# Longer pacing in the side work of a decoder layer, low parts on another engine, attention in rounds of two key blocks

## The chip, the core and the metric

The kernel runs on one core of a Trainium2 chip. Its engines work at the same time, each through its own list of instructions in order: TensorE (PE: matrix products, and transposes as products with an identity), VectorE (DVE), ScalarE (ACT), GpSimd (POOL) and SyncE (SP, which issues the transfers, DMAs). An instruction waits until what it reads is written and the buffer that it writes is free, and everything behind it in its engine's list waits too. The metric is the time of one execution in microseconds (us), as the median of several runs.

## What is computed

One layer of a hybrid decoder, 1024 tokens of width 1024 in f32:

```python
u = rmsnorm(h, norm_mix)
(... q, k, v, gates of three branches ..., mg) = split_cols(u @ w_in, IN_SIZES)
y_a = gated_deltanet(...)          # 4 heads, chunks of 64, a triangular solve per chunk
y_b = mlstm(...)                   # 4 heads, chunks of 64
y_c = nsa(...)                     # 8 heads: compressed, selected and window attention
br = einsum('bsnc,ncd->bsnd', stack([y_a, y_b, y_c]), w_branch)
merged = sum(sigmoid(mg) * br)
h = h + merged @ w_out
gt, up = split(rmsnorm(h, norm_ffn) @ w_ffn_in, 2)
h = h + (silu(gt) * up) @ w_ffn_out
h = h + sigmoid(rmsnorm(h, norm_ple) @ w_ple_gate) * (p @ w_ple_proj)
```

The window branch sees the last 512 tokens, the selected branch up to four key blocks of 64 per query; three sigmoid gates per head weigh the three outputs. The delta rule needs the inverse of a unit lower triangular 64x64 matrix for each head and chunk.

## The kernel before

**Products.** Every large product is made of three in a rounded format. Each factor is split into a high part (ScalarE copies it into the rounded type) and a low part (the difference), and hi x hi + hi x lo + lo x hi is accumulated in PSUM. So `mm<-u,whi` and `mm<-u,wlo` in the profile are products of the activations with the high and the low part of a weight tile. Weights come by DMA in tiles of 128x512 (`wraw`, four buffers); `halve` in `run_blocks` makes `whi` on ScalarE (L429) and `wlo` on GpSimd (L431), into five buffers each. In the last phase every second `wlo` is made on VectorE.

**Three phases.** (1) The input projection, block by block, with the side work of the branches woven in: the delta rule's solve (`gdn_solve`) and scan, the mLSTM, the preparation of the attention. (2) The attention (`nsa_attend`), woven into ten blocks of the merge gates (`mg_block`). (3) The remaining merge gates, the branch projections, the output projection, the feed-forward network (FFN) and the gated embedding (PLE), without side work. The FFN multiplies blocks with seven products in place of eight: the function around L1755 (called the combine here) first forms sums of activation blocks (`uw`), and `part` makes high and low parts of them (`utT1h`, `utT1l` and so on, L1763 and L1764).

**The order.** Side work is written as generators. After each step of a block `advance` adds 1.4 us to a counter, `woven`, and lets the generators issue a few pieces. `yield from self.pause(us)` makes a generator sit still until `woven` has grown by that much. So a pause puts more of the blocks' products between one piece and the next in the engines' lists; it is no wait on the chip. A scheduler then fixes the order of each engine's list before the program runs. In phase 3, `self.later(lag, fn)` holds back the issue of some work until so many us of products have been issued.

**The solve.** For each head, `gdn_solve` transposes keys and queries (`ktr`, after `g_junk`, L838), forms `gram`, inverts the 16x16 diagonal blocks on VectorE by substitution (`zb`, `xb`, L893 and L894), which takes two trips through DRAM (`zds`, `xds`) and ends in `gV` on GpSimd and `gW` on VectorE (both L908). After `pause(14.0)` the doubling follows: levels of 64x64 products, `levq`, `levv` and `levw`, which put the inverse together from the blocks. In the preparation of the attention `khtr` transposes keys (`nsa_keys`, L1261).

**The attention.** For each block of 128 queries there are four tasks: the window and the selected branch, each in two halves of the heads (`hp`). `att_query` normalises and splits the queries (`qstk`, L1387 and L1388) and transposes them (`qtr`). `att_scores` forms scores `S` and exponentials `P` with their sums `n_sum`, and scales P by gate / sum (L1476 and L1478). `att_values` works on the task before: for each key block it transposes four P tiles into one PSUM bank (`ptr`, tag "pt", two banks), copies the bank to `PT` (ScalarE and VectorE in turn, from a pool of ten buffers), and one key block later adds the products with the values to `nso`, two products of 64 columns' width. At the end the compressed branch adds `nso<-PT,cv`, two products of 64x64. `nsa_attend` interleaves the pieces of scores and values.

**FFN and PLE.** `put` makes high and low parts, `ahi` (ScalarE, L1795) and `alo` (GpSimd, L1796), of the activations for the down product. In the PLE, `evac` multiplies (VectorE, L1965), adds the residual on GpSimd (L1967) and stores. `load_y` loads a branch's output and splits it into `yhi` and `ylo` on ScalarE and VectorE at once.

## Time and profile before

| | us |
|---|---|
| median of three runs (2393.13 to 2399.14) | 2394.88 |
| the execution whose profile is shown | 2392.93 |
| its span, first to last instruction | 2391.1 |

The mean granted TensorE clock over the span is 0.987 of full speed. The stages, from the windows of the trace (busy us of each engine):

| stage | from, to (us) | PE | DVE | ACT | POOL | clock |
|---|---|---|---|---|---|---|
| input projection with side work | 0 to 880 | 826.87 | 411.25 | 298.22 | 255.32 | 0.97 |
| attention with merge gates | 880 to 1311 | 410.35 | 321.94 | 212.41 | 107.22 | 1.00 |
| merge gates, branch projections | 1311 to 1480 | 164.84 | 86.78 | 46.92 | 43.67 | 1.00 |
| output projection, norm | 1480 to 1580 | 96.06 | 59.77 | 43.20 | 22.27 | 0.99 |
| combine and FFN | 1580 to 2298 | 703.20 | 414.00 | 220.37 | 309.53 | 0.99 |
| PLE | 2298 to 2391.1 | 84.90 | 44.49 | 35.13 | 44.88 | 0.99 |

How to read the lines below: a line names the line of the kernel, the engine, the operation, out<-in, the shape and the count ("x4"). In a group the busy time, the mean ns of one, and the idle time before it with its releaser follow. In a timeline the start and the duration stand ahead, in us. In a window the length stands first, then busy us and instructions of PE, its weight loads (PEld), DVE, ACT and POOL, then the granted clock, the DMA share and GB/s. A product of f32 operands, such as `nso`, stands in the trace as two passes for each product of the instruction list.

### The profile page before, as it was taken

Reading aid. Unit: us, or ns where it says so; the run is one execution under the profiler, and the core shown is the slowest. Engines: PE = TensorE matmul, PEld = TensorE weight load, DVE = VectorE, ACT = ScalarE, POOL = GpSimd, SP = SyncE. Lnnn points to the kernel's source line nnn. Section 1 sums busy time; section 2 is a strip of 40 time slices with the busy share of each in tenths; the row PEclk is TensorE's granted clock in tenths of the full one; section 3 lists DMA queues with packets and bytes.
Section 4 is the critical chain, followed back from the end, with each engine's and each line's share of the span. In section 5 each row is a group of like instructions: output and inputs, shape, how many; then the busy total and the mean of one; then the engine's idle time right before and its main releaser. Section 6 shows DMA issues by size and latency. Waiting matters only on the chain.

```text
span 2391.1 us, 34586 instructions
## 1 busy us (share of the span) xinstructions
PE 2286.2 (96%) x12840; PEld 1829.4 (77%) x12840; DVE 1338.2 (56%) x3088; ACT 856.3 (36%) x1832; POOL 782.9 (33%) x662
## 2 busy tenths in 40 slices
PE   8989898989999998999999999998999999999999
PEld 6777677878778996666665778986777777777789
DVE  5455555643223436888775446677555555555583
ACT  6424242423222334545454322452222222222362
POOL 2342424322122123322121151235444444444434
PEclk9999999999999999999999999999999999999999
DMA  6131212121122123111111643311111111111143
GB/s 230 50 96 40 92 40 65 59 64 45 63 77 80 45 93 107 58 54 45 50 45 50 228 164 129 128 57 36 53 49 54 49 49 51 51 53 53 53 133 128
DMA packets 121887, 183.05 MB, mean 77 GB/s; under 512 B 25275, under 2 KB 47204, under 8 KB 121720
## 3 DMA queue, kind: packets, MB, share of 16 engines
q1 hardware_dynamic: 121432, 180.72, 22.5%
q8 instruction: 101, 1.65, 0.3%
q14 instruction: 66, 0.54, 0.1%
q10 hardware_dynamic: 288, 0.14, 0.0%
HBM read 149.04 MB, written 31.76 MB: 76 GB/s over the span
## 4 chain that ended last, share of the span: by engine, by line
PE 77%; DVE 12%; issue 4%; POOL 3%; DMA 3%; ACT 2%; SPq 0%; POOLq 0%; ACTq 0%; DVEq 0%
PE mm L242 60%; PE nso L242 3%; PE ptr L250 2%; PE S L242 2%; POOL wlo L431 2%; DVE P L1478 1%; DVE zb L893 1%; DVE xb L894 1%; PE mops L242 1%; PE gks L242 1%; PE gpu L242 1%; ACT g_junk L838 1%; POOL alo L1796 1%; ACT whi L429 1%; PE levq L242 1%
## 5 line engine op out<-in xcount | busy, mean ns | idle before, releaser
L431 POOL TENSOR_TENSOR wlo<-wraw,whi 128x512 fp32r<-128x512 f32 x334 | 449.7, 1351 | 1063.9 <-ACT whi L429 818.9
L242 PE MATMUL mm<-u,whi 128*128 128x512 f32 x1888 | 632.7, 410 | 2.0 <-ACT mg L1606 2.0
L429 ACT ACTIVATE whi<-wraw 128x512 fp32r<-128x512 f32 x408 | 255.7, 630 | 470.2 <-PE mm L242 384.0
L242 PEld LDWEIGHTS mm<-u,whi 128*128 128x128 f32 x1888 | 341.4, 190 | 76.0 <-issue 11.5
L242 PE MATMUL mm<-u,wlo 128*128 128x512 f32 x944 | 379.2, 402 | 0.0
L242 PEld LDWEIGHTS mm<-u,wlo 128*128 128x128 f32 x944 | 178.3, 189 | 39.4 <-issue 1.2
L1839 DVE TENSOR_TENSOR fc<-fc,mm 128x512 f32<-128x512 f32 x140 | 95.3, 686 | 159.0 <-PE mm L242 158.9
L1880 DVE TENSOR_TENSOR h<-h,mm 128x512 f32<-128x512 f32 x176 | 118.6, 684 | 74.6 <-PE mm L242 72.1
L242 PE MATMUL mm<-whi,alo 128*128 128x512 f32 x352 | 141.6, 402 | 6.8 <-POOL alo L1796 6.8
L242 PE MATMUL mm<-whi,ahi 128*128 128x512 f32 x352 | 140.7, 400 | 5.5 <-ACT whi L429 5.5
L242 PE MATMUL mm<-wlo,ahi 128*128 128x512 f32 x352 | 140.6, 399 | 2.5 <-POOL wlo L431 2.5
L431 POOL TENSOR_TENSOR wlo<-ws,whi 128x512 fp32r<-128x512 f32 x60 | 84.3, 1405 | 148.7 <-ACT whi L429 148.7
L242 PE MATMUL mm<-u2hi,whi 128*128 128x512 f32 x304 | 121.1, 398 | 0.0
L242 PE MATMUL mm<-u2lo,whi 128*128 128x512 f32 x304 | 121.1, 398 | 0.0
L242 PE MATMUL mm<-u2hi,wlo 128*128 128x512 f32 x304 | 120.3, 396 | 0.0
L1472 ACT ACTIVATE P<-P,n_ng 128x640 f32<-128x640 f32 (+7 forms) x128 | 93.0, 728 | 64.1 <-DVE n_ng L1470 61.1
L429 ACT ACTIVATE whi<-ws 128x512 fp32r<-128x512 f32 x60 | 37.8, 630 | 174.9 <-DVE h L1880 130.4
L250 PE MATMUL ptr<-ident,P 128*128 128x128 f32 x528 | 89.8, 282 | 7.3 <-DVE P L1478 5.5
L250 PEld LDWEIGHTS ptr<-ident,P 128*128 128x128 f32 x528 | 59.6, 140 | 47.2 <-issue 28.3
L242 PE MATMUL mm<-whi,u 128*128 128x256 f32 x512 | 94.1, 283 | 0.1
L431 DVE TENSOR_TENSOR wlo<-wraw,whi 128x512 fp32r<-128x512 f32 x74 | 69.5, 939 | 35.5 <-ACT whi L429 35.4
L242 PEld LDWEIGHTS mm<-whi,alo 128*128 128x128 f32 x352 | 66.8, 190 | 27.2 <-POOL alo L1796 11.6
(497 smaller groups left out, 5048.9 us busy)
## 6 DMA issues: line engine op xcount, KB each, us to landing
wraw<-in_w_dram SPq DMA_DIRECT2D x408, 256.0 KB, 2.7
mgs<-mg SPq DMA_DIRECT2D x48, 256.0 KB, 2.3
mgld<-mgs SPq DMA_DIRECT2D x48, 256.0 KB, 5.6
xt<-in_x_dram SPq DMA_DIRECT2D x8, 512.0 KB, 4.8
xt<-in_x_dram SPq DMA_DIRECT2D x32, 128.0 KB, 3.7
sg<-pps SPq DMA_DIRECT2D x32, 128.0 KB, 3.5
out_dram<-sg SPq DMA_DIRECT2D x32, 128.0 KB, 2.8
pps<-ppst SPq DMA_DIRECT2D x8, 256.0 KB, 2.0
```

What stands on the lines that cost most here:

```text
L242: return self.nc.tensor.matmul(out, lhsT, rhs, start=start, stop=stop).ins
L250: self.nc.tensor.transpose(out, in_, self.ident[:n, :n])
L429: nc.scalar.activation(hi, t, AF.Copy)
L431: eng.tensor_tensor(lo, t, hi.bitcast(F32), OP.subtract)
L838: nc.scalar.activation(junk, ps[:, q * P:q * P + P], AF.Square, accum_out=ssq[:, w, 4 * hf + q:4 * hf + q + 1])
L893: nc.vector.tensor_tensor(tmp[:, :m, m:], bc(Z[:, :m, m:m + 1], shp), bc(X[:, m:m + 1, m:], shp), OP.mult)
L894: nc.vector.tensor_tensor(X[:, :m, m:], X[:, :m, m:], tmp[:, :m, m:], OP.subtract)
L1472: nc.scalar.activation(pts[i][:, :nk], pts[i][:, :nk], AF.Exp, bias=ng[:, i:i + 1], accum_out=sm[:, g, i % 2:i % 2 + 1])
L1478: nc.vector.tensor_scalar(pts[i][:, :nk], pts[i][:, :nk], sm[:, g, i % 2:i % 2 + 1], None, OP.mult)
L1796: nc.gpsimd.tensor_tensor(lo, t, hi.bitcast(F32), OP.subtract)
L1839: nc.vector.tensor_tensor(t, x, ps, OP.add)
L1880: nc.vector.tensor_tensor(self.h[tt][s], self.h[tt][s], ps, OP.add)
```

## The change

It has three parts. **Pacing:** the pause ahead of the doubling goes from 14 to 24, the one behind the second operand's `ktr` steps from 1.4 to 3, that in the first half of `khtr` from 3 to 6. **Low parts:** the sixteen of the combine, part of those of the FFN's activations, and the PLE's residual sums go from GpSimd to VectorE; `load_y` issues its splits by `later`, except for the loads marked `first`. **Attention:** `att_values` transposes two key blocks and then multiplies the two before; the pieces of values and scores interleave differently; `att_query` is split in two and issued during the task ahead; the gate moves into the scaling of P as a second factor; `cv` is laid out with zeros beside it, so that one product of full width takes the place of two.

```diff
 COMBINE_LAG = 8.0
+Y_LAG = 9.0
...
                     nc.scalar.activation(junk, ps[:, q * P:q * P + P], AF.Square,
                                          accum_out=ssq[:, w, 4 * hf + q:4 * hf + q + 1])
-                yield from self.pause(1.4)
+                yield from self.pause(3.0 if w else 1.4)
...
         for eng, M, w in ((nc.gpsimd, V, 0), (nc.vector, W, 1)):
             eng.tensor_tensor(M.rearrange("p t (d i) -> p t d i", d=4), bc(d3(1 + w).unsqueeze(2), [P, NT, 4, 16]),
                               bc(self.blk4.unsqueeze(1).unsqueeze(3), [P, NT, 4, 16]), OP.mult)
-        yield from self.pause(14.0)
+        yield from self.pause(24.0)
...
                 nc.scalar.activation(hl[0][:, :, :, w], k4, AF.Copy)
             for w in range(2):
                 nc.vector.tensor_tensor(hl[1][:, :, :, w], k4, hl[0][:, :, :, w].bitcast(F32), OP.subtract)
-            yield from self.pause(3.0)
+            yield from self.pause(6.0 if hf == 0 else 3.0)
...
-        cv = self.small("cv", [P, 64])
+        cv = self.small("cv", [P, 2, 64])
...
-            dst = ckr if n == "k" else cv
             ps = self.ps("ncmp")
...
             for g in range(2):
-                nc.vector.tensor_copy(dst[64 * g:64 * g + 63], ps[64 * g:64 * g + 63, :64])
+                rows = slice(64 * g, 64 * g + 63)
+                nc.vector.tensor_copy(ckr[rows] if n == "k" else cv[rows, g], ps[rows, :64])
...
         prev = None
-        for t in tasks + [None]:
+        for _ in self.att_query(0):
+            pass
+        for n, t in enumerate(tasks + [None]):
             a = self.att_scores(*t) if t else iter(())
+            after = (tasks + [None] * 2)[n + 1]
             b = self.att_values(prev) if prev else iter(())
             cur = None
-            nb = prev["nb"] + 2 if prev else 0
+            nb = -(-prev["nb"] // 2) + 2 if prev else 0
             done = 0
             for i in range(4):
                 cur = next(a, None) or cur
                 yield
-                upto = -(-nb * (i + 1) // 4)
+                upto = -(-nb * i // 3)
                 while done < upto:
                     if next(b, 0) is None:
                         yield
                     done += 1
+                if after and after[0] == "w" and after[2] == 0:
+                    if i == 0:
+                        ahead = self.att_query(after[1])
+                        next(ahead)
+                    elif i == 3:
+                        next(ahead)
             prev = cur
 
     def att_query(self, qt):
...
             hs = slice(4 * g, 4 * g + 4)
             nc.scalar.activation(s[:, hs, g], q[:, hs], AF.Copy)
             nc.vector.tensor_tensor(s[:, hs, 1 - g], q[:, hs], s[:, hs, g].bitcast(F32), OP.subtract)
-        out = []
+        yield
+        out = st["qT", qt] = []
         qT = self.a4("qT", F32R, "x")
         for g in range(2):
             ps = self.ps("qtr", "pt")
...
             t = qT[:, 512 * g:512 * g + 512]
             nc.scalar.activation(t, ps, AF.Copy)
             out.append(t)
-        return out
+        yield
 
     def att_scores(self, br, qt, hp):
 
         if br == "w" and hp == 0:
-            st["qT", qt] = self.att_query(qt)
             st["pc", qt] = self.b2("pc")
...
                                          accum_out=sm[:, g, i % 2:i % 2 + 1])
                 nc.vector.tensor_scalar(sm[:, g], sm[:, g], 1e-30, None, OP.max)
                 nc.vector.reciprocal(sm[:, g], sm[:, g])
-                nc.vector.tensor_tensor(sm[:, g], sm[:, g], gate[:, g], OP.mult)
                 for i in (n - 1, n):
-                    nc.vector.tensor_scalar(pts[i][:, :nk], pts[i][:, :nk], sm[:, g, i % 2:i % 2 + 1], None, OP.mult)
+                    nc.vector.tensor_scalar(pts[i][:, :nk], pts[i][:, :nk], sm[:, g, i % 2:i % 2 + 1],
+                                            gate[:, g, i % 2:i % 2 + 1], OP.mult, OP.mult)
             if br == "w" and hp == 0 and n in CMP_AT:
                 next(cmp_)
             if n < 3:
...
         cols = slice(256 * hp, 256 * hp + 256)
         v = st["v" + br]
         nb = t["nb"]
-        pend = None
-        for kb in range(nb + 1):
-            if kb < nb:
+        pend = []
+        for kb in range(0, nb + 2, 2):
+            new = []
+            for b in range(kb, min(kb + 2, nb)):
                 ps = self.ps("ptr", "pt")
                 for n in range(4):
-                    self.tr(ps[:, n * P:n * P + P], pts[n][:, kb * P:kb * P + P])
+                    self.tr(ps[:, n * P:n * P + P], pts[n][:, b * P:b * P + P])
                 pt = self.b2("PT")
-                if kb % 2 == 1:
+                if b % 2 == 1:
                     nc.vector.tensor_copy(pt, ps)
                 else:
                     nc.scalar.activation(pt, ps, AF.Copy)
-            if pend is not None:
-                b, pt_ = pend
+                new.append((b, pt))
+            for b, pt_ in pend:
                 for g in range(2):
                     vv = v[:, (k0 + b) * P + 64 * g:(k0 + b) * P + 64 * g + 64]
                     self.mm(o[64 * g:64 * g + 64, cols], vv, pt_[:, 256 * g:256 * g + 256],
                             br == "w" and hp == 0 and b == 0, False)
-            pend = (kb, pt) if kb < nb else None
+            pend = new
             yield
         if br == "s":
 
...
                 self.tr(ps[:, n * P:n * P + P], pc[:, h * P:h * P + P])
             ct = self.b2("PT")
             nc.vector.tensor_copy(ct[:, :256], ps[:, :256])
-            for g in range(2):
-                gp = slice(64 * g, 64 * g + 64)
-                self.mm(o[gp, cols], st["cv"][gp], ct[gp, :256], False, hp == 1)
+            self.mm(o[:, cols], st["cv"].rearrange("p g d -> p (g d)"), ct[:, :256], False, hp == 1)
         if br == "s" and hp == 1:
             yo = self.s2("yo")
             nc.scalar.activation(yo, o, AF.Copy)
...
         return (self.chan_block(self.u, evac, hfs=(half,)), ("mg", b))
 
     def load_y(self, src, scale, first):
+
         nc = self.nc
         res = {}
+        def parts(kk, hf, t):
+            hi, lo = self.l2("yhi", F32R), self.l2("ylo", F32R)
+            self.split(hi, lo, t, scale)
+            res[kk, hf] = (hi, lo)
         for hf in range(2):
             for kk in range(4):
                 t = self.l2("yld")
                 dma = nc.sync.dma_start(t, src[kk, :, hf * 512:hf * 512 + 512])
                 if first:
                     self.tc.keep_in_program_order(dma)
-                hi, lo = self.l2("yhi", F32R), self.l2("ylo", F32R)
-                self.split(hi, lo, t, scale)
-                res[kk, hf] = (hi, lo)
+                    parts(kk, hf, t)
+                else:
+                    self.later(Y_LAG + 2.56 * (4 * hf + kk), lambda kk=kk, hf=hf, t=t: parts(kk, hf, t))
         return res
 
     def branch_blocks(self):
...
         def part(n, t, pool=None):
             hi, lo = self.l2("ut" + n + "h", F32R, pool), self.l2("ut" + n + "l", F32R, pool)
             nc.scalar.activation(hi, t, AF.Copy)
-            nc.gpsimd.tensor_tensor(lo, t, hi.bitcast(F32), OP.subtract)
+            nc.vector.tensor_tensor(lo, t, hi.bitcast(F32), OP.subtract)
             self.ub[n][k] = hi, lo
 
         def whole(pair):
...
         blocks = []
 
         def put(f, hf, t):
             hi, lo = self.l2("ahi", F32R), self.l2("alo", F32R)
             nc.scalar.activation(hi, t, AF.Copy)
-            nc.gpsimd.tensor_tensor(lo, t, hi.bitcast(F32), OP.subtract)
+            (nc.vector if f < 2 or f % 2 and hf == 0 else nc.gpsimd).tensor_tensor(lo, t, hi.bitcast(F32), OP.subtract)
             act[f, hf] = (hi, lo)
 
         def gate(ct, hf, ps):
...
                 nc.scalar.activation(t, ps[:, :256], AF.Sigmoid)
                 nc.vector.tensor_tensor(t, t, pp, OP.mult)
                 h = self.h[tt][c // 2][:, cs]
-                nc.gpsimd.tensor_tensor(t, t, h, OP.add)
+                nc.vector.tensor_tensor(t, t, h, OP.add)
                 nc.sync.dma_start(self.out[tt * P:tt * P + P, c * 256:c * 256 + 256], t)
             return f
 
```

The first place where the order moves is the solve of the first head. GpSimd's list around `gV`, before and then after (the numbers tell tiles apart; `wlo_1430` to `wlo_1442` are the low parts of the same block of weights in both):

```order
L431 TENSOR_TENSOR wlo_1332<-wraw_1203,whi_1331 128x512
L431 TENSOR_TENSOR wlo_1430<-wraw_1335,whi_1429 128x512
L908 TENSOR_TENSOR gV_1382<-zd_1300,c128_135 128x512
L431 TENSOR_TENSOR wlo_1434<-wraw_1337,whi_1433 128x512
L431 TENSOR_TENSOR wlo_1438<-wraw_1339,whi_1437 128x512
L431 TENSOR_TENSOR wlo_1442<-wraw_1341,whi_1441 128x512
```

After the change, the same stretch of GpSimd's list:

```order
L432 TENSOR_TENSOR wlo_1299<-wraw_1182,whi_1298 128x512
L432 TENSOR_TENSOR wlo_1430<-wraw_1302,whi_1429 128x512
L432 TENSOR_TENSOR wlo_1434<-wraw_1304,whi_1433 128x512
L432 TENSOR_TENSOR wlo_1438<-wraw_1306,whi_1437 128x512
L909 TENSOR_TENSOR gV_1410<-zd_1352,c128_135 128x512
L432 TENSOR_TENSOR wlo_1442<-wraw_1308,whi_1441 128x512
L432 TENSOR_TENSOR wlo_1510<-wraw_1445,whi_1509 128x512
```

Three low parts of this block stood behind `gV`; now one does. TensorE's list where the doubling begins in the same head, before:

```order
L242 MATMUL mm_1453<-u_433,wlo_1332 128x512
L242 MATMUL mm_1540<-u_301,whi_1319 128x512 x2
L242 MATMUL mm_1540<-u_301,wlo_1320 128x512
L242 MATMUL mm_1540<-u_309,whi_1319 128x512 x2
L242 MATMUL levq_1483<-gW_1383,zak_1250 64x64 x8
L242 MATMUL levq_1483<-gW_1383,zak_1276 64x64 x8
```

And TensorE's list there after:

```order
L243 MATMUL mm_1561<-u_600,whi_1441 128x512 x2
L243 MATMUL mm_1561<-u_600,wlo_1442 128x512
L243 MATMUL mm_1561<-u_618,whi_1441 128x512 x2
L243 MATMUL mm_1561<-u_618,wlo_1442 128x512
L243 MATMUL levq_1589<-gW_1411,zak_1278 64x64 x8
L243 MATMUL levq_1589<-gW_1411,zak_1328 64x64 x8
```

Counted in this list, 89 products of 512 columns stood between the second `gram` and `levq` in the first head (89, 90 and 90 in the others). Now 132 do in each, and the products with `wlo_1442` stand ahead of `levq`, no longer behind it.

The second place is the attention, a window task of five key blocks. TensorE's list before (a row `nso ... x2` holds the two products of one key block):

```order
L242 MATMUL nso<-PT,nvw 64x256 x2
L250 MATMUL ptr<-ident,P 128x128 x4
L242 MATMUL nso<-PT,nvw 64x256 x2
L250 MATMUL ptr<-ident,P 128x128 x4
L242 MATMUL S<-khh,qT 128x256
L242 MATMUL S<-kll,qT 128x256
L242 MATMUL S<-khh,qT 128x384
L242 MATMUL S<-kll,qT 128x384
```

And after, in a task of the same size:

```order
L251 MATMUL ptr<-ident,P 128x128 x4
L243 MATMUL nso<-PT,nvw 64x256
L251 MATMUL ptr<-ident,P 128x128 x4
L243 MATMUL nso<-PT,nvw 64x256 x3
L243 MATMUL S<-kll,qT 128x384
L243 MATMUL S<-khh,qT 128x256
L243 MATMUL S<-kll,qT 128x256
L251 MATMUL ptr<-ident,P 128x128 x4
L243 MATMUL nso<-PT,nvw 64x256 x6
```

Products with the values now stand in larger groups. Counted over the program, 126 visits of TensorE to `nso` with `nvw` or `nvs` become 85, and the 471 products of the merge gates that stand within the attention become 382.

The third place is the FFN: VectorE's list around the end of a block of seven products, before:

```order
L1839 TENSOR_TENSOR fc<-fc,mm 128x512 x2
L1857 TENSOR_TENSOR fc<-fc 128x512
L1839 TENSOR_TENSOR fc<-fc,mm 128x512
L1880 TENSOR_TENSOR h<-h,mm 128x512
L1862 TENSOR_TENSOR fc<-fc 128x512
```

And after:

```order
L1859 TENSOR_TENSOR fc<-fc,mm 128x512 x2
L1877 TENSOR_TENSOR fc<-fc 128x512
L1816 TENSOR_TENSOR alo<-fc,ahi 128x512
L1859 TENSOR_TENSOR fc<-fc,mm 128x512
L1900 TENSOR_TENSOR h<-h,mm 128x512
L1882 TENSOR_TENSOR fc<-fc 128x512
```

`alo` now stands on VectorE right behind the product that it is made from, ahead of the next sum with a PSUM bank.

More of the change, by code (lines that the diff above doesn't have):

```diff
@@ L1336, in nsa_compress @@
         self.dump("ck", ckr)
-        self.dump("cv", cv)
         yield
```

## The prediction

> **What bounds the kernel now.** I read the profile's page first, the busy time and the chain that ended last:
>
> ```profile
> PE 2286.2 (96%) x12840; PEld 1829.4 (77%) x12840; DVE 1338.2 (56%) x3088; ACT 856.3 (36%) x1832; POOL 782.9 (33%) x662
> ...
> PE 77%; DVE 12%; issue 4%; POOL 3%; DMA 3%; ACT 2%; SPq 0%; POOLq 0%; ACTq 0%; DVEq 0%
> ```
>
> TensorE (PE) is busy for 2286.2 of 2391.1 us, so about 105 us are idle, and a change that takes away next to no products can win little more than that, plus what the clock loses after long stalls. Second, TensorE's waits (releaser: us in total, times, longest):
>
> ```profile
> PE levq L242 <- DVE gW L908: 30.0, 4, 8.5
> PE mm L242 <- POOL alo L1796: 6.8, 11, 1.7
> PE mm L242 <- POOL wlo L431: 6.2, 7, 2.5
> PE qtr L248 <- DVE qstk L1388: 6.2, 8, 1.7
> PE mm L242 <- ACT whi L429: 5.5, 1, 5.5
> PE ptr L250 <- DVE P L1478: 5.5, 12, 0.8
> ...
> PE khtr L248 <- ACT khht L1261: 3.2, 2, 1.7
> PE ktr L250 <- ACT g_junk L838: 3.0, 3, 1.3
> ...
> PE mm L242 <- DVE acc L1658: 1.2, 1, 1.2
> ```
>
> Nearly every edit points at one of these rows. So I price each by the row it points at, and then ask what is late next.
>
> **Pause 14 to 24 ahead of the doubling (L908).** One of the four heads, from the timeline (start, us; idle before in brackets), and two products 19 products apart, in a stretch without a wait:
>
> ```profile
> 130.05 1.06 PE L242 MATMUL gram<-gq,kT 128*128 128x128 f32 x8
> ...
> 157.94 1.04 POOL L908 TENSOR_TENSOR gV<-zd,c 128x512 f32<-128x512 f32 x1 [10.79 <-DMA zd<-xds]
> 159.67 1.97 PE L242 MATMUL levq<-gW,zak 64*64 64x64 f32 x32 [7.85 <-DVE gW L908]
> ...
> 162.50 1.27 POOL L431 TENSOR_TENSOR wlo<-wraw,whi 128x512 fp32r<-128x512 f32 x1 [3.52 <-PE mm L242]
> ...
> 1618.62 0.39 PE L242 MATMUL mm<-u2hi,wlo 128*128 128x512 f32 x1
> ...
> 1623.05 0.40 PE L242 MATMUL mm<-whi,ahi 128*128 128x512 f32 x1
> ```
>
> From the last gram's end (131.1) a serial chain of small VectorE work and two trips through DRAM takes 26.8 us to gV and 28.6 us to levq. In the order TensorE has only 89 products of 512 columns to do meanwhile. One takes (1623.05 - 1618.62) / 19 = 0.233 us from start to start, so that is 20.7 us, and it stands still for the rest. In the changed order 132 products, 30.8 us, stand between gram and levq in each head. That is 2.2 us more than the chain needs, so the wait itself goes. The clock after such stalls (windows; the last figures are the granted clock, the DMA share and GB/s):
>
> ```profile
> 159.60:164.40 4.80, 4.73 (x52) 3.80 (x54) 0.69 (x1) 0.00 (x0) 1.27 (x1) 0.50 0.00 0
> 278.60:283.80 5.20, 5.17 (x60) 4.24 (x62) 0.69 (x1) 0.00 (x0) 1.27 (x1) 0.50 0.00 2
> 396.40:400.00 3.60, 3.54 (x36) 2.97 (x36) 0.69 (x1) 0.00 (x0) 0.00 (x0) 0.51 0.00 0
> 503.00:509.00 6.00, 6.00 (x76) 5.04 (x78) 0.69 (x1) 0.00 (x0) 0.00 (x0) 0.50 0.01 3
> 180.00:240.00 60.00, 58.69 (x303) 47.21 (x302) 35.55 (x75) 24.23 (x76) 13.94 (x16) 1.00 0.11 40
> ```
>
> In the first four TensorE works through 19.6 us at half clock; half of that, 9.8 us, is lost beside the 30.0 us of idle. Per head that is 10.3, 11.1, 8.7 and 9.8 us.
>
> What is late next is on GpSimd, which issues in order. In the first head the changed order puts gV ahead of wlo_1442, and TensorE reads wlo_1442 first 104 products (24.2 us) behind the gram. gV is ready only at 26.8 + 1.04, and the low part behind it (1.27) at 29.1: some **4.9 us** of wait come back there. What the clock does behind 4.9 us no row shows exactly: behind the four stalls the loss was 1.8 to 3.0, behind a ktr wait of 1.3 (in the fifth window) nothing, so between 0 and 3; I take 2, near the stalls it resembles. In the other heads the low parts behind gV are read 134 products (31.2 us) or more behind the gram, later than 29.1. So the heads give 3.4 + 11.1 + 8.7 + 9.8 = **33 us**.
>
> The Trainium skill, "TensorE: Matmul & The Clock Gate", section "What's actually happening", says that the TensorE clock falls to half after an idle window of about 3.4 us. The four windows agree (0.50 after stalls of 6.8 to 8.5 us); by that rule the remaining 4.9 us would be followed by a half-clock stretch, and the sum would have 3 in place of my 2.
>
> **Pauses ahead of ktr and khtr.** The ktr transposes wait 3.0 us; 3.0 in place of 1.4 us of pacing covers the longest wait, 1.3: **3**. khtr waits 3.2, but its place moves by only 0.7 to 1.9 us of products in the order: **2**. Later places of side work are absorbed by the products behind them: in the order the side work ends 3 us of products later, with over 50 us of products still behind it.
>
> **Attention.** Rows from the timeline, the groups and the windows:
>
> ```profile
> 962.22 0.65 PE L242 MATMUL nso<-PT,cv 64*64 64x256 f32 x4
> ...
> 1005.71 0.60 PE L250 MATMUL ptr<-ident,P 128*128 128x128 f32 x4
> 1006.07 0.48 PE L242 MATMUL S<-khh,qT 128*128 128x512 f32 x1
> ...
> 1063.98 0.66 PE L250 MATMUL ptr<-ident,P 128*128 128x128 f32 x4
> 1064.56 0.65 PE L242 MATMUL nso<-PT,nvw 128*64 128x256 f32 x4
> ```
>
> ```profile
> L1478 DVE TENSOR_SCALAR P<-P,n_sum 128x640 f32<-128x640 f32 (+7 forms) x128 | 70.5, 591 | 0.8
> L1476 DVE TENSOR_TENSOR n_sum<-n_sum,cgate 128x2 f32<-128x2 f32 x64 | 19.4, 304 | 0.7
> ...
> L1722 DVE TENSOR_SCALAR xn<-h,rsq_yna 128x512 f32<-128x512 f32 x32 | 17.5, 590 | 0.2
> ...
> 1020.00:1080.00 60.00, 56.73 (x324) 36.74 (x324) 52.79 (x199) 31.40 (x73) 15.86 (x16) 1.00 0.14 49
> ...
> 920.00:1308.90 388.90, 370.23 (x2137) 242.31 (x2135) 310.47 (x1143) 198.49 (x443) 91.97 (x89) 1.00 0.15 50
> ```
>
> Four transposes between full-width products take 0.36 us (1005.71 to 1006.07); between two visits of the 64-column nso they take 0.58. A visit saved is worth about 0.2 us. The order has 126 such visits before and 85 after: 41 x 0.2 = **8**. The cv product is one full-width product for a 0.65 us group of four passes; the S row (512 columns in 0.48) bounds what is left, and I take 0.25 saved, 16 x 0.25 = **4** (between 0 and 6). The qtr wait of 6.2 falls to about 1, since att_query is now issued a task ahead: **5**. VectorE loses L1476, 19.4 us; its factor moves into L1478 as a second operand, and L1722, which has 128x512 alone, is no dearer (590 against 591), so the cost there lies between 0 and 0.1 us each. Of the ptr waits (5.5) I give it **3**.
>
> Against this: in the order 471 products are woven into attention before and 382 after, so the stage (388.9 us) has 89 x 0.233 = 20.7 us less cover; the products follow later, at no cost of their own. VectorE, busy 52.8 of 60 us in its middle, loses some 3 of them and then stands at 49.8 / (60 x 356 / 389) = 91%, and a round holds both transposed-probability banks at once. How many new waits that makes no row shows: between 0 and about 30 us (0.4 us in each of 76 rounds). I take **8**, near the 8.5 us by which ptr and nso wait for such copies and probabilities now. Net **12**.
>
> **Low parts on VectorE, combine.** Rows of 1585 to 1640, and the longest stall:
>
> ```profile
> L1769 DVE TENSOR_TENSOR uw<-u2hi,u2lo 128x512 f32<-128x512 f32 x16 | 19.1, 1215 | 0.1
> L1764 POOL TENSOR_TENSOR utT2l<-uw,utT2h 128x512 fp32r<-128x512 f32 x4 | 7.0, 1749 | 0.0
> L1776 DVE TENSOR_TENSOR uw<-uw 128x512 f32<-128x512 f32 x4 | 2.8, 690 | 0.1
> ...
> 1631.37 0.79 PE L242 MATMUL mm<-whi,ahi 128*128 128x512 f32 x1 [5.48 <-ACT whi L429]
> ```
>
> The same two-input operation takes VectorE 0.69 us alone and up to 1.8 beside GpSimd's. Sixteen lows leave GpSimd; they add 16 x 0.69 = 11 us to VectorE, which in turn loses about (1.215 - 0.69) x 16 = 8 on L1769 and some 8 on its other sixteen. So it ends a few us sooner. The stalls there are 1.7 (alo), 5.5 (whi behind a copy that waits for VectorE) and 2.5 (wlo); the first goes, about half of the others: **6**, bounds 0 and 12.
>
> **FFN.** One of ten equal waits:
>
> ```profile
> 1760.35 1.28 POOL L1796 TENSOR_TENSOR alo<-fc,ahi 128x512 fp32r<-128x512 f32 x1 [1.29 <-ACT ahi L1795]
> ...
> 1761.69 0.50 PE L242 MATMUL mm<-whi,alo 128*128 128x512 f32 x1 [0.52 <-POOL alo L1796]
> ```
>
> TensorE comes to it at 1761.17. With 0.69 in place of 1.28 alo ends at 1761.04, just ahead: 10 x 0.5 = **5**. If GpSimd's next low runs beside it and it takes 1.6 to 1.8, the wait grows by 0.4 each: between -4 and 6.
>
> The Trainium skill, "GPSIMD Engine Reference", section "1. Specifications", says that GpSimd shares its SBUF interfaces with VectorE, with contention for instructions with two SBUF inputs. The trace agrees (1.215 against 0.69). Taken to the letter here, every alo on VectorE would run contended, and this term would be -4 in place of 5.
>
> **Rest.** The y parts are now split later (Y_LAG), so that acc no longer stands behind them: **1**. In the PLE
>
> ```profile
> L1967 POOL TENSOR_TENSOR sg<-sg,h 128x256 f32<-128x256 f32 x32 | 25.7, 803 | 43.7 <-DVE sg L1965 38.6 <-ACT u2hi L319 4.3 <-DVE rsq_yna L309 0.9
> ...
> 2319.50 0.39 PE L242 MATMUL mm<-wlo,u2hi 128*128 128x256 f32 x1 [1.79 <-POOL wlo L431]
> ```
>
> the low stood behind two such sums; on VectorE the wait goes and the last sum is shorter by about 0.4: **2**.
>
> **Sum.** 33 + 3 + 2 + 12 + 6 + 5 + 1 + 2 = 64 us. The profiled execution took 2392.93 us (its span, 2391.1, and 1.8 around it), so 2329; it lies 2 us under the median shown, 2394.88.
>
> **Rivals.**
> A. *Everything clears*: the first head's low part is not late after all (+7), attention makes no new waits (+8), combine its upper bound (+6): 2329 - 21 = 2308. For it: GpSimd's second zx stands two lows sooner in the chain now; against it: VectorE's 91%.
> B. *The wait changes its name*: gV, on GpSimd in order, holds up low parts in all heads, because the weights' DMAs arrive in another rhythm than the order lets me count. Each head then gives only 3.4: 33 becomes 14, time 2348. Against it: the 31.2 us above.
> C. *Attention gives nothing*: VectorE binds the stage; its 20 us of gains are matched by new waits up to the bound of 30: 2329 + 22 = 2351.
> D. *Slower*: both probability banks and four copies are held per round. If the copies, which stand in VectorE's queue behind 0.6 us operations on P, make TensorE wait for a bank in each of the 76 rounds, the gains of 64 + 8 = 72 us are eaten from 0.95 us a round on. At 1.2 us, a copy's wait behind two such operations, the cost is 91: time 2393 + 91 - 72 = 2412. Against it: ACT takes every second copy and is busy 31 of 60 us.
> E. *The pause doesn't move levq*: the order excludes it.
>
> **How the numbers follow.** Forecast 2329 (spread 2316 to 2342): 0.57. A 0.13, B 0.12, C 0.12, D 0.04, and 0.02 for some sum of B and C with the FFN's lower bound that ends level. The range reaches over A with the cv and FFN upper bounds (2302) and over B and C with the combine's lower bound (2357). A measurement of this kernel tells 0.3% (7 us) from no change: faster 0.94, same 0.02, slower 0.04.
>
> **What would show it.** The row levq <- gW gone, a wait for POOL wlo of some 5 us ahead of the first head's levq, clock 1.00 in the other three; nso visits unchanged in number of passes but the stage from 388 to about 355 us; alo absent from TensorE's waits, or with 10 waits of near 0.9 if contention rules; the combine stalls under 5 us in sum. A stage of attention above 370 us, or POOL waits in more than one head, would make the prediction wrong.

## The result and the profile after

The changed kernel takes 2331.09 us in the median (2326.78 to 2333.03), the kernel before 2394.01 us beside it. The ratio is 0.9731, with a 95% interval of 0.9711 to 0.9751, so the change is 63 us faster; 2329 was forecast. In the page of the changed kernel, busy time and the chain that ended last:

```profile
PE 2267.1 (97%) x12808; PEld 1834.1 (79%) x12808; DVE 1324.7 (57%) x3086; ACT 852.3 (37%) x1832; POOL 711.2 (31%) x600
...
PE 84%; DVE 10%; issue 2%; ACT 2%; DMA 1%; POOL 1%; SPq 0%; ACTq 0%; POOLq 0%; DVEq 0%
```

TensorE's idle time fell from 105 to 63 us of a span that is 61 us shorter. Busy time itself fell by 19 us: 7 of them in the attention beside the products that moved out of it, where TensorE switches less between forms of products, and some 8 in the first stage and the combine, where less of the time is at half clock (the mean granted clock rose from 0.987 to 0.996). TensorE's waits in the changed kernel (releaser: us in total, times, longest):

```profile
PE ptr L251 <- DVE P L1488: 7.9, 13, 1.1
PE gytr L251 <- DVE vtok L1013: 5.4, 2, 3.1
PE mm L243 <- POOL wlo L432: 5.1, 5, 4.1
...
PE mm L243 <- DVE acc L1677: 2.5, 1, 2.5
PE gks L243 <- DVE gS L995: 2.4, 1, 2.4
PE gpu L243 <- DVE gvn L988: 2.1, 2, 1.2
...
PE mm L243 <- ACT utT4h L1782: 2.0, 1, 2.0
...
PE khtr L249 <- ACT khht L1262: 1.5, 2, 0.8
```

`levq`, `qtr`, `ktr` and every `alo` are gone. Three names are new, `gytr`, `gks` and `gpu`: the scan of the delta rule, 9.9 us in sum. The prediction doesn't speak of them. Where the time went, by the start of the same instruction in both traces (us from the span's start):

| up to | before | after | step | forecast |
|---|---|---|---|---|
| first `qtr` (input projection, pacing) | 920.1 | 895.0 | -25.1 | -38 |
| first product with `yhi` (attention, its products included) | 1333.6 | 1295.2 | -13.3 | -12 |
| first product with `u2hi` (branches, output) | 1572.3 | 1533.6 | -0.2 | -1 |
| first product with `utT2h` (combine) | 1661.1 | 1610.4 | -12.0 | -6 |
| last product with `alo` (FFN) | 2284.9 | 2227.9 | -6.3 | -5 |
| last product (PLE) | 2386.3 | 2325.6 | -3.8 | -2 |

The sum was right to a microsecond or two, but by errors that cancel: the first stage gave 13 us less than forecast in this execution, the combine 6 more. One execution differs from the next by some microseconds in the first row: -26.2 to -28.9 in E2, E3, E4, E9, E10 and E11 below, whose edits leave this stage's pacing as it is. In the combine's row the other runs with the same combine have -8.9 to -12.0, by the stretches of 3.4 us at half clock that fall into it. Two places answer to the prediction's rows. The first head's doubling, timeline of the changed kernel (start, us):

```profile
159.75 0.63 PE L243 MATMUL mm<-u,whi 128*128 128x512 f32 x2
164.45 0.80 PE L243 MATMUL mm<-u,wlo 128*128 128x512 f32 x1 [4.08 <-POOL wlo L432]
...
161.69 1.04 POOL L909 TENSOR_TENSOR gV<-zd,c 128x512 f32<-128x512 f32 x1 [6.86 <-DMA zd<-xds]
162.69 2.94 POOL L432 TENSOR_TENSOR wlo<-wraw,whi 128x512 fp32r<-128x512 f32 x2
```

And the window behind it (length, busy us of PE, PEld, DVE, ACT and POOL, granted clock, DMA share, GB/s):

```profile
164.40:170.40 6.00, 5.95 (x14) 4.75 (x15) 0.00 (x0) 0.60 (x1) 1.23 (x1) 0.50 0.41 134
```

GpSimd does nothing for 6.86 us, because `gV` stands at the head of its list; the low part runs behind it, and TensorE waits 4.08 us for that (forecast 4.9). The clock is 0.50 for 6 us behind it, a loss of 3 (I had taken 2 of 0 to 3). The combine, a group of the changed kernel and then its timeline:

```profile
L1788 DVE TENSOR_TENSOR uw<-u2hi,u2lo 128x512 f32<-128x512 f32 x16 | 12.6, 820 | 0.0
```

```profile
1590.69 0.47 PE L243 MATMUL mm<-whi,ahi 128*128 128x512 f32 x1 [2.04 <-ACT utT4h L1782]
```

The sums of halves take 820 ns in the mean, not 1215, and of three stalls with 9.7 us one of 2.04 is left.

### The profile page after: what moved, and what is told of

The parts are those of the page before. It is cut to its first block, busy times and chain, and to the rows that moved or that the text cites. A ratio compares the mean times of both kernels' runs of the same rounds, so it can differ in the third digit from the quotient of the medians.

```text
span 2330.0 us, 34428 instructions
## 1 busy us (share of the span) xinstructions
PE 2267.1 (97%) x12808; PEld 1834.1 (79%) x12808; DVE 1324.7 (57%) x3086; ACT 852.3 (37%) x1832; POOL 711.2 (31%) x600
## 4 chain that ended last, share of the span: by engine, by line
PE 84%; DVE 10%; issue 2%; ACT 2%; DMA 1%; POOL 1%; SPq 0%; ACTq 0%; POOLq 0%; DVEq 0%
PE mm L243 68%; PE nso L243 3%; PE ptr L251 2%; PE S L243 2%; DVE P L1488 1%; PE mops L243 1%; PE gpu L243 1%; PE gks L243 1%; PE gram L243 1%; DVE P L1477 1%; POOL wlo L432 1%; DVE uw L1788 0%; DVE xn L1741 0%; PE u2tr L251 0%; PE levv L243 0%
## 5 line engine op out<-in xcount | busy, mean ns | idle before, releaser
L432 POOL TENSOR_TENSOR wlo<-wraw,whi 128x512 fp32r<-128x512 f32 x334 | 442.9, 1332 | 1036.0 <-ACT whi L430 773.7
L243 PEld LDWEIGHTS mm<-whi,alo 128*128 128x128 f32 x352 | 66.3, 188 | 18.7 <-DVE alo L1816 3.2
```

The source lines that it names most:

```text
L243: return self.nc.tensor.matmul(out, lhsT, rhs, start=start, stop=stop).ins
L432: eng.tensor_tensor(lo, t, hi.bitcast(F32), OP.subtract)
```

## The experiments

Each ran on the chip beside the kernel before; times are medians. Edits are against the changed kernel.

**E1, the long pause alone undone.**

```diff
-        yield from self.pause(24.0)
+        yield from self.pause(14.0)
```

> The changed kernel with the pause ahead of the doubling back at 14. Theory of the ledger: the four levq waits return (30 us idle and 10 at half clock), the 4 us wait for the low part behind gV goes with its 3 of clock, and the waits of the scans (gytr, gks, gpu: 10 us idle and 3 of clock) go as well, so the kernel takes about 2331 + 20 = 2351 us. Rival, the prediction's term: the pause alone was worth 33, so 2364. Second rival: the scans' waits have nothing to do with the pause and stay, then 2331 + 33 = 2364 with the gytr waits of some 5 us still in the trace.

Measured: 2343.85 us, 12.8 slower than the changed kernel, ratio 0.9789 (0.9775 to 0.9804). None of the three numbers fits. The row of the waits:

```profile
PE levq L243 <- DVE gW L909: 20.7, 4, 8.3
```

The four waits return with 20.7 us, not 30: 7.3 and 8.3 in the first two heads, 3.2 and 1.9 in the others. In these two the chain from `gram` to `gV` has become shorter, as the table under E5 shows. Its cause must be another part of the change.

**E2, all moved low parts and sums back on GpSimd.**

```diff
-            nc.vector.tensor_tensor(lo, t, hi.bitcast(F32), OP.subtract)
+            nc.gpsimd.tensor_tensor(lo, t, hi.bitcast(F32), OP.subtract)
...
-            (nc.vector if f < 2 or f % 2 and hf == 0 else nc.gpsimd).tensor_tensor(lo, t, hi.bitcast(F32), OP.subtract)
+            nc.gpsimd.tensor_tensor(lo, t, hi.bitcast(F32), OP.subtract)
...
-                nc.vector.tensor_tensor(t, t, h, OP.add)
+                nc.gpsimd.tensor_tensor(t, t, h, OP.add)
```

> The changed kernel with all the moved low parts and the PLE's sums back on GpSimd. Ledger by stages: combine +12, FFN +6, PLE +4, so 2353 us. Rival, the prediction's terms (6 + 5 + 2): 2344. If VectorE's operations in the combine are slow because GpSimd works beside them, the uw sums of two halves take about 1.2 us in the mean again (0.82 in the changed kernel); if they were only queued late, they stay at 0.8.

Measured: 2349.38 us, 18.3 slower, ratio 0.9814 (0.98 to 0.9829): between the two, nearer to the ledger. By the same landmarks the combine loses 10.4 us, the FFN 6.3, the PLE 2.3. Rows of E2, the waits and then groups of the window 1546 to 1605 (one of the sixteen sums falls outside):

```profile
PE mm L243 <- POOL alo L1816: 6.5, 11, 1.7
PE mm L243 <- ACT whi L430: 5.5, 1, 5.5
```

```profile
L1788 DVE TENSOR_TENSOR uw<-u2hi,u2lo 128x512 f32<-128x512 f32 x15 | 18.4, 1251 | 0.1
...
L1797 DVE TENSOR_TENSOR uw<-uw 128x512 f32<-128x512 f32 x4 | 7.1, 1780 | 0.1
```

The same sums on VectorE take 1251 ns again although nothing was edited in them; only GpSimd works beside them. E2 brings back the slower low parts and their company at once, so it doesn't tell the two apart. In the kernel before, the stall of 5.48 us ended with a `whi` that stood on ScalarE behind a copy of a sum which had taken VectorE 1.81 us. So I read most of the combine's gain as VectorE freed from GpSimd's company, not as sixteen operations done faster; that wasn't tried by itself.

**E3, the whole attention as before** (the functions `nsa_attend`, `att_query`, `att_scores`, `att_values` and the layout of `cv` of the kernel before).

> The changed kernel with the whole attention as before. Ledger: the stage with its products gave 13 us, so 2344 us; attention alone then lasts about 389 us instead of 355, with 471 products in it. Rival: the 13 us come from the weights and transfers arriving in another rhythm after the first stage, not from the attention's code; then 2331 to 2335.

Measured: 2346.31 us, 15.2 slower, ratio 0.98 (0.9785 to 0.9815). The attention's windows, E3 and then the changed kernel (length, busy PE, PEld, DVE, ACT, POOL, clock):

```profile
892.10:1281.90 389.80, 370.41 (x2134) 242.43 (x2134) 310.28 (x1143) 198.43 (x443) 91.98 (x89) 1.00 0.15 50
```

```profile
895.00:1250.10 355.10, 342.46 (x2016) 237.51 (x2015) 294.75 (x1077) 193.01 (x433) 85.04 (x84) 1.00 0.15 48
```

The stage is 389.8 us long again, against 355.1 (about 355 was forecast); of the 34.7 us, 20.7 are products that come later. Of the other 14.0, 6.8 are idle time of TensorE (length less busy time, 19.4 against 12.6) and 7.2 busy time. The attention's gain is its own code.

**E4, y split at once, as before.**

```diff
-                    parts(kk, hf, t)
-                else:
-                    self.later(Y_LAG + 2.56 * (4 * hf + kk), lambda kk=kk, hf=hf, t=t: parts(kk, hf, t))
+                hi, lo = self.l2("yhi", F32R), self.l2("ylo", F32R)
+                self.split(hi, lo, t, scale)
+                res[kk, hf] = (hi, lo)
```

> The changed kernel with the splits of y issued at once. Theory: the wait of acc in the branch stage is for the load of the merge gates (mgld), not for the splits ahead of it, so nothing is gained by the lag: 2330 to 2332, and the acc wait stays between 1 and 3 us. Rival, the prediction's: the splits held acc up, so 1 to 3 us slower, with an acc wait longer than 2.5 us.

Measured: 2330.9 us, ratio 0.9737 (0.972 to 0.9753): no difference. The `acc` wait is still there and no longer than the 2.5 us of the changed kernel, as the theory says. Its row in E4, and then VectorE's timeline in the changed kernel, which shows what it is for:

```profile
PE mm L243 <- DVE acc L1669: 1.6, 1, 1.6
...
1311.08 2.01 DVE L1677 SCALAR_TENSOR_TENSOR acc<-mgld,mm 128x512 f32<-128x512 f32 x3 [13.89 <-DMA mgld<-mgs]
```

It waits for a load of the merge gates. The lag removed nothing; its term was 1 us too much.

**E5, all three pauses as before.**

```diff
-                yield from self.pause(3.0 if w else 1.4)
+                yield from self.pause(1.4)
...
-        yield from self.pause(24.0)
+        yield from self.pause(14.0)
...
-            yield from self.pause(6.0 if hf == 0 else 3.0)
+            yield from self.pause(3.0)
```

> The changed kernel with all three pauses as before (14, 1.4, 3). Theory: the pause of ktr did more than its own 3 us: by moving the side work it also lets the second zx run at once and keeps GpSimd's low parts out of part of the triangle's loop on VectorE, so that the chain from gram to levq got shorter by 1 to 6 us a head. Then with it undone the chain is 27.7 to 29.2 us long again in every head, the levq waits are 30 us in sum (20.7 with the pause of 14 alone undone), the loop takes 11 us in each head, and the time is 2331 + 25 = 2356 us. Rival: the shorter chain of heads 2 and 3 is chance or comes from another part of the change; then the waits stay near 21 us and the time is 2331 + 13 + 5 = 2349.

Measured: 2360.98 us, 29.9 slower, ratio 0.9856 (0.9841 to 0.9872). The wait is whole again:

```profile
PE levq L243 <- DVE gW L909: 30.4, 4, 8.3
```

So undoing the long pause costs 12.8 us, undoing all three 29.9. Per head, from the traces, the time from the end of the last `gram` to `gV`, and the length of the loop over the triangle (`zb`, `xb`) within it:

| | to `gV`, heads 1 to 4 (us) | loop (us) | operations over 0.7 us, of 30 |
|---|---|---|---|
| before | 26.8, 27.5, 26.1, 26.0 | 11.0, 11.3, 10.9, 11.1 | 4, 4, 4, 4 |
| E5 | 26.8, 27.2, 26.7, 25.9 | 11.2, 11.2, 11.0, 11.1 | 4, 4, 4, 4 |
| E1 | 25.4, 27.5, 22.4, 21.1 | 12.2, 13.2, 8.7, 7.2 | 5, 6, 2, 0 |
| changed | 25.5, 27.5, 22.6, 20.1 | 12.3, 12.8, 8.8, 7.0 | 5, 6, 2, 0 |

The two shorter pauses change the chain itself. Every one of the slow operations runs beside one of GpSimd's, which had started first, and none of the 120 is slow without it. Two stretches of such a loop, the kernel before (GpSimd, then VectorE):

```profile
141.46 2.74 POOL L431 TENSOR_TENSOR wlo<-wraw,whi 128x512 fp32r<-128x512 f32 x2 [3.73 <-ACT whi L429]
...
141.52 1.29 DVE L893 TENSOR_TENSOR zb<-zb,xb 64x39 f32<-64x39 f32 x1
142.84 0.19 DVE L894 TENSOR_TENSOR xb<-xb,zb 64x39 f32<-64x39 f32 x1
143.07 1.19 DVE L893 TENSOR_TENSOR zb<-zb,xb 64x48 f32<-64x48 f32 x1
```

And the changed kernel's last head, where GpSimd is silent throughout:

```profile
490.83 0.22 DVE L894 TENSOR_TENSOR zb<-zb,xb 64x63 f32<-64x63 f32 x1
491.08 0.22 DVE L895 TENSOR_TENSOR xb<-xb,zb 64x63 f32<-64x63 f32 x1
```

An operation of 0.2 us that meets a low part of 1.3 us sits it out. Which low parts fall into the loop depends on where the side work stands among the blocks, and that is what the pause of `ktr` shifts; the `khtr` of `nsa_keys` start at 800.8 us in the changed kernel, behind the last of these loops. The second `zx` also runs 0.4 us behind `gram` now, not 1.6 to 1.7.

**E6, gV on VectorE; E7, gytr later; E8, both.**

```diff
-        for eng, M, w in ((nc.gpsimd, V, 0), (nc.vector, W, 1)):
+        for eng, M, w in ((nc.vector, W, 1), (nc.vector, V, 0)):
```

```diff
-        yield from self.pause(8.0)
+        yield from self.pause(14.0)
```

> The changed kernel with gV on VectorE behind gW, so that no low part stands behind it on GpSimd. Theory: the 4 us wait for wlo in the first head goes, and some 3 us of half clock after it; levq needs gW alone, so nothing takes its place: 2331 - 6 = 2325 us. Rival: the low part is late for another reason (its weights or its buffer), then the wait stays and the time is 2331.

> The changed kernel with the pause ahead of gytr at 14 in place of 8. Theory: after the change only 5.4 to 5.6 us of products stand between a scan's end and gytr in the first two heads (9.8 before), while the chain through rsqrt and vtok takes 9; the two waits of 5.4 us go, with 1.7 us of half clock: 2331 - 6 = 2325 us. Rival: VectorE is late there by itself, the wait moves to the next reader of the scan: 2331.

> The two edits before this together. Theory: they are in different places and add: 2331 - 12 = 2319 us, idle of the first stage some 9 us less than the changed kernel's. Rival: what one frees the other waits for, and they give no more than one: 2325.

Measured: 2325.52 us (ratio 0.9709, 0.9695 to 0.9723), 2323.97 us (0.9705, 0.9692 to 0.9719) and 2318.41 us (0.968, 0.9666 to 0.9693). The two alone give 5.6 and 7.1, together 12.7: they add, as expected. In E6 the long wait for the low part is gone and `gytr` stays; in E7 the low part's wait stays and no row of `gytr` is left:

```profile
PE ptr L251 <- DVE P L1488: 7.9, 13, 1.1
PE gytr L251 <- DVE vtok L1013: 5.4, 2, 3.1
...
PE mm L243 <- POOL wlo L432: 1.0, 4, 0.3
```

```profile
PE ptr L251 <- DVE P L1488: 7.8, 13, 1.1
...
PE mm L243 <- POOL wlo L432: 4.7, 5, 3.6
```

E8 is the fastest kernel of the study, 12.7 us below the changed one and with an interval that doesn't touch its own.

**E9, rounds of one key block.**

```diff
-            nb = -(-prev["nb"] // 2) + 2 if prev else 0
+            nb = prev["nb"] + 2 if prev else 0
...
-        for kb in range(0, nb + 2, 2):
+        for kb in range(nb + 1):
...
-            for b in range(kb, min(kb + 2, nb)):
+            for b in range(kb, min(kb + 1, nb)):
```

> The changed kernel with rounds of one key block in att_values; att_query ahead, cv in one product and the folded gate stay. TensorE's visits to nso go from 85 back to 130 and 471 products of the merge gates are woven in again (382). Theory, the prediction's term of 0.2 us a visit: 2331 + 9 = 2340 us. Rival: VectorE binds the stage, so that fewer visits are worth nothing: 2331 within 3 us. Second rival: the rounds are all of the stage's gain: 2331 + 13 = 2344, with new waits for PT or ptr besides.

Measured: 2340.83 us, 9.7 slower, ratio 0.978 (0.9765 to 0.9795), as the term of 0.2 us a visit says. By the landmarks of its one trace the stage is only 7.6 us longer. Its attention's window:

```profile
893.90:1277.50 383.60, 369.56 (x2105) 247.27 (x2104) 301.49 (x1079) 198.14 (x443) 93.33 (x89) 1.00 0.15 51
```

It is 28.5 us longer than the changed kernel's, 20.7 of them products that come sooner. Of the other 7.8, 1.4 are idle time (14.0 against 12.6) and 6.4 busy time, with a stretch of 3.4 us at half clock among it (from 957.6 on). So 45 more visits cost TensorE busy time rather than waits, and a visit is worth 0.22 us by the medians, 0.14 by this trace, and 0.10 if the 1.7 us that the stretch can have cost are taken off.

**E10, att_query not ahead** (it runs through at the start of its own task).

```diff
-        for _ in self.att_query(0):
-            pass
...
-                if after and after[0] == "w" and after[2] == 0:
-                    if i == 0:
-                        ahead = self.att_query(after[1])
-                        next(ahead)
-                    elif i == 3:
-                        next(ahead)
...
         if br == "w" and hp == 0:
+            for _ in self.att_query(qt):
+                pass
```

> The changed kernel with att_query issued at the start of its own task, as before. Theory: the qtr waits come back, about 6 us in sum, and the time is 2331 + 5 = 2336 us. Rival: other waits of the same moment (ptr, S) hid them, then 2331 to 2333.

Measured: 2359.16 us, 28.1 slower, ratio 0.9865 (0.9847 to 0.9882). Far more than either theory. Its waits and its attention's window:

```profile
PE qtr L249 <- DVE qstk L1391: 17.1, 10, 3.4
```

```profile
893.70:1281.30 387.60, 356.90 (x2030) 250.04 (x2028) 303.87 (x1077) 191.71 (x433) 85.10 (x84) 0.97 0.13 44
```

The `qtr` wait is 17.1 us, not the 6.2 of the kernel before; TensorE is idle for 30.7 us of that stage (387.6 less 356.9) against 12.6, which makes 18. With stalls up to 3.4 us the granted clock falls to 0.97 over 387.6 us, some 10 us more. So the two edits of the attention depend on each other: with rounds of two and the later values of the task before, the queries' own chain lies open unless it is issued a task ahead. That fewer products stand in front of `qtr` then is my reading of the code and wasn't tried by itself.

**E11, two products for cv.**

```diff
-            self.mm(o[:, cols], st["cv"].rearrange("p g d -> p (g d)"), ct[:, :256], False, hp == 1)
+            for g in range(2):
+                gp = slice(64 * g, 64 * g + 64)
+                self.mm(o[gp, cols], st["cv"][gp, g], ct[gp, :256], False, hp == 1)
```

> The changed kernel with two products of 64x64 for cv in place of one of full width (the layout with zeros stays). Theory: 16 groups cost 0.25 us more each, 2331 + 4 = 2335 us. Rival: the group's time is hidden or the switch costs less: 2331 to 2333.

Measured: 2332.89 us, 1.8 slower, ratio 0.9749 (0.9735 to 0.9764), which overlaps the changed kernel's. By the landmarks of its one trace the stage is 4.4 us longer, but a stretch at half clock lies in it. Between 0 and 4 us stays open.

**E12, the long pause alone kept.**

```diff
-                yield from self.pause(3.0 if w else 1.4)
+                yield from self.pause(1.4)
...
-            yield from self.pause(6.0 if hf == 0 else 3.0)
+            yield from self.pause(3.0)
```

> The changed kernel with the pauses of ktr and khtr as before; the one ahead of the doubling stays at 24. Theory: the two pauses are two ways to the same 30 us and not parts that add. The chain from gram to levq is 28 to 29 us again, but 132 products (30.8 us) cover it, so the levq waits stay at 0; ktr and khtr wait 6 us again, and low parts behind gV are read 116 and 110 products behind the gram in the first two heads, so that waits for wlo of about 2 and 4 us are there: 2331 + 7 = 2338 us. Rival, parts that add: pause 24 is worth only the 13 us that undoing it cost, so 2361 - 13 = 2348.

Measured: 2331.29 us, the same as the changed kernel, ratio 0.9739 (0.9722 to 0.9755). The waits:

```profile
PE mm L243 <- POOL wlo L432: 6.8, 6, 3.2
PE u2tr L251 <- DVE u2lo L321: 4.7, 3, 2.0
...
PE khtr L249 <- ACT khht L1262: 3.2, 2, 1.7
PE gks L243 <- DVE gS L995: 2.9, 2, 2.4
```

The mechanism is as expected: no `levq` wait, two low parts late behind `gV` (5.8 us of the 6.8; 2 and 4 were expected), `khtr` back at 3.2. But `ktr` waits only 0.4, and the scans' `gytr` 0.3 in place of 5.4, so it costs nothing in sum. Parts that add would have given 2348.

Why `gytr` doesn't wait here shows in the chain of the first head's scan. The same operation, in the changed kernel and then in E12:

```profile
227.85 1.31 DVE L297 SCALAR_TENSOR_TENSOR rsq_tgo<-rsq_tgo,g_s 128x8 f32<-128x8 f32 x1
```

```profile
220.47 0.17 DVE L297 SCALAR_TENSOR_TENSOR rsq_tgo<-rsq_tgo,g_s 128x8 f32<-128x8 f32 x1
```

In the changed kernel, 4 and 3 of the 11 operations of `rsqrt` and its last factor take 1.1 to 1.3 us in the first two heads, each beside a low part on GpSimd, and `gytr` starts 8.7 and 7.7 us behind the scan. In E12 all 11 take 0.17 us, and it starts 4.5 and 4.9 us behind. It is the effect of E5's loop in another chain.

## Why the prediction came out right, step by step

- **Pacing, 33 + 3 + 2 = 38: measured 25 in the profile, 30 by E5. This step was mis-sized.** The `levq` wait and its half clock went as said, and the low part behind `gV` cost 4.1 us in the one head that was named, at the place and for the reason given (E6). What failed is the question "what is late next": I searched the lists of GpSimd and stopped there. The scan of the same head is late next too. From its end to `gytr` stand 5.6 and 5.4 us of products in the first two heads in the changed order, where 9.8 stood in both, and its chain through `rsqrt` takes 8.7 and 7.7, lengthened by GpSimd (E12). That, `gks` and `gpu` are 9.9 us of waits, with two stretches of 3.4 us at half clock. E7 takes the larger part back. What makes `gks` and `gpu` late stays open.
- **The pauses as separate terms: wrong.** The long pause alone gives all 30 (E12). The short ones alone give 17 of them (E5 against E1), not 5: 9.7 us of the `levq` waits (30.4 to 20.7) beside 4.9 of `ktr` and `khtr`, with less half clock behind them. They do it by taking low parts out of the serial loop in two heads and letting the second `zx` run 1.2 us sooner in all four. So they are largely two ways to one wait. And where both stand, `gytr` and `gpu` wait 7.5 us, in E12 0.3, which takes back what the short ones save.
- **Attention, 12: measured 13.3, 15.2 by E3.** The sum held, its parts less so. The working had 12 of busy time (visits 8, `cv` 4) and waits that cancel (5 and 3 against 8). The windows before and after have 7.0 less busy time, beside the 20.7 us of products, and 6.0 less idle time (18.7 to 12.6). The visits are between 4.7 and 9.7 (E9). For `qtr` I had 5; 6.2 of waits went, and without `att_query` ahead this form of the stage is 28 us longer, so that price holds for the old form alone. `cv`, 4, is between 0 and 4. The 8 us charged for new waits were too many: the `ptr` waits for P rose from 5.5 to 7.9 and didn't fall by the 3 given to them, those for copies (`PT`) fell. VectorE is busy 52.4 of 60 us in the middle of the stage (1020 to 1080), 87% and not 91%. The gate as a second factor isn't free: the scalings of P, the same forms in the same numbers, take 606 ns in the median where 545 were taken, within the 0 to 0.1 us given to it. L1722, which suggested no cost, has a constant of the code as its second factor.
- **Combine, 6: measured 12.0, and 10.4 by E2.** The stated upper bound was the truth. The window of this row, before and after:

```profile
1572.30:1661.00 88.70, 77.03 (x322) 60.95 (x321) 73.37 (x109) 33.82 (x73) 45.35 (x30) 0.92 0.12 39
```

```profile
1533.60:1610.40 76.80, 72.81 (x323) 58.34 (x322) 68.97 (x130) 34.05 (x73) 14.72 (x10) 1.00 0.14 46
```

VectorE ends "a few us sooner" as worked out: it is busy 4.4 us less with the low parts on it. What the step mis-sized is what that gives TensorE. It took 5.7 of the 9.7 us of stalls for gone, and 7.7 went. And it had no term for the clock, which rose from 0.92 to 1.00 and makes 4.2 us of busy time. Part of that is luck: the stall of 2.04 us that is left wasn't followed by half clock here, nor in E4, E6 and E10. In E1, E3, E5, E7, E9, E11 and E12 the same stall was followed by a stretch of 3.4 us, and the step is -10.3 to -10.5.
- **FFN, 5: measured 6.3.** Ten low parts run in 0.69 us each on VectorE, none slowed, and the wait is gone. The result of -4 that the prediction set beside it did not come. **PLE, 2: 3.8 and 2.3 by E2. Branches, 1: 0** (E4).
- **Rivals.** B was right as a mechanism in one head and wrong in the others; E12 shows it in two. C and D, attention that gives nothing or costs time, are refuted by E3 and E9. A's conditions were half met: no more waits in attention than before and the combine at its bound, but the first head not clear. The lower end of the range, 2302, doesn't follow from its own bounds: 2308 less 2 for `cv` and 1 for the FFN is 2305.

The forecast held to 2 us because the combine and the PLE gave back what the scans took. That is luck in the sum, not in the mechanisms.

## What to carry to other kernels

When a serial chain is hidden behind a pause, list everything that follows in the same stream, up to its last output, and give each its own distance; here the wait moved to places that had only just been covered. Price pauses and lags together, since two of them can hide the same wait, and one can change the length of the chain by moving another engine's work out of it. Before counting an engine's operations at their own duration, look at what runs beside them.

## What the runs showed of the hardware that was not expected

**A two-input operation of VectorE waits out one of GpSimd that started first, whatever its own size.** One of 64x39 took 1.29 us beside a low part, and 0.19 us alone; sums of 128x512 took 1.25 us in the mean in E2 and 0.82 in the changed kernel. Of the loops' 120 operations, 16 were over 0.7 us before, 13 after, all of them beside a GpSimd operation that had started first. The Trainium skill, "SBUF — State Buffer", section "SBUF: two separate sides", says that the port pair that the two share is an exclusive lock: whichever operation starts first has it to its end, and the other is blocked. The loop's rows agree, and so do E2's. By that rule it is the start that decides, which fits the ten `alo` on VectorE that kept their 0.69 us: in nine of them a low part of GpSimd starts 0.57 us behind them.

**Half clock after short stalls.** A `gks` wait of 2.40 us was followed by a granted clock of 0.50, in the windows of the changed kernel (the 3.4 us up to there, and those behind):

```profile
423.00:426.40 3.40, 1.00 (x5) 0.50 (x4) 1.67 (x4) 2.32 (x4) 1.13 (x2) 1.00 0.00 0
426.40:429.80 3.40, 3.40 (x12) 2.92 (x13) 2.66 (x4) 0.77 (x3) 0.00 (x0) 0.50 0.00 0
```

In E1 the `levq` wait of 3.2 us was followed by such a stretch, the one of 1.9 us was not; in the changed kernel neither the `acc` wait of 2.50 us nor a `gytr` wait of 2.35 was, and the `utT4h` stall of 2.0 to 2.1 us was followed by one in some runs alone (above), so the length of the stall alone doesn't decide. The Trainium skill, "TensorE: Matmul & The Clock Gate", section "What's actually happening", speaks of an idle window of about 3.4 us; here 2.4 us of idle time was enough.
